# Attention value products by head: two 64-column products in place of one 128-column product, and one copy per result

## Chip, core and metric

The kernel runs on one core of a Trainium2 chip. The metric is the device time of one execution in microseconds (us); less is better. Engines: TensorE (PE in the profile, with its weight loads as PEld), VectorE (DVE), ScalarE (ACT), GpSimd (POOL) and SyncE (SP, which issues most loads).

## What is computed

The reference is a two-layer encoder over 512 positions and 1024 channels. Each layer adds three branches to the residual and then a squared-ReLU MLP. Branch C, which the change touches, is windowed grouped-query attention with 8 query heads of 64 columns and 2 key/value heads; a block of 128 queries sees its own block of 128 keys and the two beside it:

```
scores = jnp.einsum('bnqhgd,bnkhd->bnhgqk', qb, kb).astype(jnp.float32) * (C_HDIM ** -0.5)
...
p = p / (jnp.sum(p, axis=-1, keepdims=True) + jnp.exp(sink_l - m))
o = jnp.einsum('bnhgqk,bnkhd->bnqhgd', p.astype(v.dtype), vb)
```

The change concerns the last line, probabilities times values. All of it is in float32.

## The kernel before

A layer first projects its input (the matmuls of lines 201 to 203 and 407 to 409), then works out the branches. Branch A is a gated recurrence in four heads. Branch B is a gated product, whose columns `fill` merges one after another (`merge_b`, tiles gz and yB). Branch C is attention. After that come the branches' output projections (yC, yA), the output projection (wo) and the MLP (up and the d tiles). Large products are made from three matmuls of split operands, 128 weight columns by 512 moving columns each.

Branch C takes its 8 heads as four pairs, j = 0 to 3: head j of the first key/value head with head 4 + j, which belongs to the second. The pair's 2 × 64 channels stand on the 128 partitions of one tile: the first head ("lo64") on partitions 0 to 63, the second ("hi64") on 64 to 127. The values cv have keys on partitions and the two value heads side by side in 128 columns. For each pair and each block n of 128 queries, `c_scores` (line 903) makes the scores of both heads (lines 914 and 915), the softmax (917 to 925) and the scaled probabilities, head 0 on DVE (928) and then head 1 on ACT (930). `c_out` (line 933) turns them and multiplies them by the values:

- line 943: PE transposes each key block of head 0 into a PSUM tile, then those of head 1;
- line 944: ACT copies each head's turned blocks to the SBUF tile pT, which holds, per key block, head 0's 128 query columns and then head 1's;
- line 948: for each of the 2 or 3 key blocks b, one matmul with all 128 value columns as weights and both heads' 256 columns moving, summed over b in the PSUM tile po (128 partitions × 256 columns);
- line 950: two ACT copies, each of 64 partitions × 128 columns, take the two useful quarters of po to yc: head 0's value columns with head 0's probabilities, and the same of head 1. The other two quarters, each head's probabilities with the other's values, are not used.

There are 32 such results, 4 pairs × 4 query blocks × 2 layers. The end blocks see 2 key blocks and the inner ones 3, so 10 per pair and 80 in all. In float32 each non-transposing matmul of the program stands in the profile as two rows, so line 948 has 160.

Branch A's heads (`a_head`, line 528) run beside this. Their line 540 makes products with 64 weight columns and 64 moving columns, two for each of four position tiles, written to partitions 0 to 63 and 64 to 127 by turns, eight per call of `attn`; each head calls it eight times.

The order on each engine is not written by hand. The kernel is traced in program order with priorities (`later` puts a part behind others), and a scheduler at build time places instructions of the branches between one another on every engine. PSUM tiles come from four pools of two banks; the turned probabilities, po and some others share pool "s". The tile pT has one buffer, so the next result's copies of line 944 wait for the products that read it.

Of the kernel before, what the change touches and what calls it, by code (L numbers as in the profile page):

```python
# [12 lines left out]
P = 128  # L13
# [46 lines left out]
def trunk(tc, xT, xt, ws, vec, fnb, bsb, snk, wst, rope, cmask, amask, ident, out):  # L60
    nc = tc.nc
# [30 lines left out]
    def nm(s):  # L92
        ctr[0] += 1
        return f"{s}_{ctr[0]}"

    def T(tag, name, dt=F32):
        where = part[HOME[tag]] if tag in HOME else sb
        return where.tile([P, S], dt, tag=tag, bufs=SLOTS[tag], name=nm(name))
# [17 lines left out]
    def PT(tag, name):  # L116
        return ps.tile([P, S], F32, tag="p_" + tag, bufs=BANKS[tag], name=nm(name))
# [561 lines left out]
    for l in range(DEPTH):  # L679
# [194 lines left out]
        lo64, hi64 = slice(0, 64), slice(64, 128)  # L874
# [15 lines left out]
        cv = T("ch", "cvt")  # L890
# [10 lines left out]
        yc = []  # L901
# [31 lines left out]
        def c_out(j, n, lo_, nb, Ps):  # L933
            if n == 0:
                yc.append(T("l", "yc"))


            pT = part["br"].tile([P, 3, 2, P], F32, tag="pT", bufs=1, name=nm("pT"))
            for h in range(2):
                pt = PT("s", "pT")  # L940
                for b in range(nb):
                    c = slice(b * P, (b + 1) * P)
                    nc.tensor.transpose(pt[:, c], Ps[h][:, c], id_t)
                nc.scalar.copy(pT[:, :nb, h], pt[:, :nb * P].rearrange("p (a b) -> p a b", a=nb))
            po = PT("s", "po")
            for b in range(nb):
                kb = (lo_ + b) * P
                nc.tensor.matmul(po[:, 0:2 * P], cv[:, kb:kb + P], pT[:, b].rearrange("p a b -> p (a b)"), start=b == 0, stop=b == nb - 1)  # L948
            for h, r in enumerate((lo64, hi64)):
                nc.scalar.copy(yc[j][r, n * P:(n + 1) * P], po[r, h * P:(h + 1) * P])  # L950

        def gates(tag, i, fl):

# [12 lines left out]
        def c_run(j):  # L966
            nonlocal prev
            with later(15000):
                qs = c_q(j)
                for n in range(4):  # L970
                    cur = c_scores(j, n, qs)
                    if prev is not None:
                        c_out(*prev)
                    prev = cur
# [13 lines left out]
        with later(15000):  # L988
            c_out(*prev)
# [281 lines left out]
```

## Time and profile before

| What | Value |
|---|---|
| Three runs | 1712.42, 1714.54, 1716.99 us; median 1714.54 us |
| Profiled execution, its own time | 1714.73 us |
| Span of its instructions | 1712.9 us, 22985 instructions |
| Mean granted clock of TensorE | 0.994 |

In the profile, a row of a group of instructions gives line, engine, operation, output tile<-input tiles, shape and count, then the busy time in us and the mean of one in ns, and behind the second bar the idle time of the engine before them and what ended it. For PE "128\*64" means 128 rows and 64 weight columns in use. A row of the timeline gives start and duration in us, and "x4" where equal instructions were merged: the duration then runs from the first one's start to the last one's end. PE's matmuls overlap, so what one costs is the distance from its start to the start of the next. A row of the windows gives, for a stretch, each engine's busy time with the number of instructions, then the granted PE clock, the DMA share and the transfer rate.

Branch C's products run in two stretches, from about 250 to 440 us in the first layer and from about 1100 to 1284 us in the second.

### The profile page before, as it was taken

To read this page: it belongs to the slowest core of one execution; us is meant where nothing else is said; L and a number is where in the kernel's file an instruction comes from. 1 tells how busy PE (TensorE), PEld (TensorE's weight loads), DVE (VectorE), ACT (ScalarE), POOL (GpSimd) and SP (SyncE) were. 2 spreads that over 40 slices of the span, in tenths; PEclk is the share of its full clock that TensorE was granted. 3 is DMA by queue.
4 is the path that set the end of the run, shared out by engine and by line. 5 is a ranking of instruction groups with operands and counts; after the bars stand their busy time and mean duration, and the time that the engine had idled before them with its cause. 6 is when DMAs were issued, how large, how long until landed. Compare 5 with 4: busy or idle time off the path is not lost.

```text
span 1712.9 us, 22985 instructions
## 1 busy us (share of the span) xinstructions
PE 1675.5 (98%) x8536; PEld 1379.8 (81%) x8536; DVE 1285.7 (75%) x2049; ACT 1009.5 (59%) x1691; POOL 122.0 (7%) x198
## 2 busy tenths in 40 slices
PE   7999999999999999999999999999999999999997
PEld 5788887887778888888878888888877788888886
DVE  7896987678465758687889869876875567676877
ACT  6565578677325645455666666877882355545464
POOL 1021000000320000000010210000004100000001
PEclk9999999999999999999999999999999999999999
DMA  8243222231465233332333332322216453232311
GB/s 318 77 148 108 87 87 87 87 105 56 156 237 184 88 122 98 100 111 99 123 123 98 136 106 84 105 87 87 98 44 248 158 185 99 99 112 85 124 61 50
DMA packets 58144, 199.85 MB, mean 117 GB/s; under 512 B 7888, under 2 KB 8144, under 8 KB 58032
## 3 DMA queue, kind: packets, MB, share of 16 engines
q1 hardware_dynamic: 44496, 154.46, 27.0%
q0 software_dynamic: 13248, 43.40, 6.9%
q8 instruction: 67, 1.10, 0.3%
q10 hardware_dynamic: 288, 0.52, 0.1%
q14 instruction: 45, 0.37, 0.1%
HBM read 177.38 MB, written 20.97 MB: 116 GB/s over the span
## 4 chain that ended last, share of the span: by engine, by line
PE 86%; ACT 5%; DVE 4%; DMA 2%; issue 1%; POOL 1%; SPq 0%; POOLq 0%; ACTq 0%; DVEq 0%
PE up L202 7%; PE up L201 7%; PE up L203 7%; PE dA L408 3%; PE dA L407 3%; PE dA L409 3%; PE po L948 2%; PE gA L407 2%; PE wo L244 2%; PE at L540 2%; PE dC L408 2%; PE dC L407 2%; PE dC L409 2%; PE gA L409 2%; PE gA L408 2%; PE wo L243 2%
## 5 line engine op out<-in xcount | busy, mean ns | idle before, releaser
L196 ACT CAST wh<-wq 128x1024 fp32r<-128x1024 f32 x196 | 206.3, 1052 | 213.5 <-PE dA L408 49.2
L196 ACT CAST wh<-wr 128x1024 fp32r<-128x1024 f32 x171 | 179.6, 1050 | 247.5 <-PE up L202 88.7
L197 DVE TENSOR_TENSOR wl<-wr,wh 128x1024 fp32r<-128x1024 f32 x171 | 208.8, 1221 | 154.2 <-ACT wh L196 153.3
L197 DVE TENSOR_TENSOR wl<-wq,wh 128x1024 fp32r<-128x1024 f32 x196 | 239.0, 1221 | 89.0 <-ACT wh L196 87.8
L202 PE MATMUL up<-xl,wh 128*128 128x512 f32 x512 | 199.1, 389 | 0.0
L203 PE MATMUL up<-xh,wl 128*128 128x512 f32 x512 | 199.0, 389 | 0.0
L201 PE MATMUL up<-xh,wh 128*128 128x512 f32 x512 | 198.6, 389 | 0.0
L201 PEld LDWEIGHTS up<-xh,wh 128*128 128x128 f32 x512 | 96.1, 188 | 20.1
L203 PEld LDWEIGHTS up<-xh,wl 128*128 128x128 f32 x512 | 96.1, 188 | 20.0
L202 PEld LDWEIGHTS up<-xl,wh 128*128 128x128 f32 x512 | 96.1, 188 | 19.7
L407 PE MATMUL dA<-wh,sh 128*128 128x512 f32 x256 | 99.7, 390 | 0.0
L408 PE MATMUL dA<-wh,sh 128*128 128x512 f32 x256 | 99.6, 389 | 0.0
L409 PE MATMUL dA<-wl,sh 128*128 128x512 f32 x256 | 92.6, 389 | 0.0
L580 DVE TENSOR_TENSOR ex<-ex 128x512 f32<-128x512 f32 x112 | 74.8, 685 | 4.7 <-ACT kt L556 4.2
L407 PEld LDWEIGHTS dA<-wh,sh 128*128 128x128 f32 x256 | 48.0, 188 | 10.0
L409 PEld LDWEIGHTS dA<-wl,sh 128*128 128x128 f32 x256 | 48.1, 188 | 10.0
L408 PEld LDWEIGHTS dA<-wh,sh 128*128 128x128 f32 x256 | 48.1, 188 | 9.9
L263 POOL TENSOR_TENSOR rs<-ms,mhalf_t 128x4 f32<-128x4 f32 (+2 forms) x15 | 18.5, 1233 | 493.6 <-DVE ms L261 484.3
L554 DVE TENSOR_TENSOR qt<-qt,q 128x512 f32<-128x512 f32 x56 | 38.4, 686 | 18.9 <-ACT qt L553 18.5
L553 ACT ACTIVATE qt<-ex 128x512 f32<-128x512 f32 x56 | 37.7, 674 | 24.5 <-DVE ex L580 19.4
L251 ACT CAST sh<-sf 128x512 fp32r<-128x512 f32 x64 | 39.6, 619 | 19.4 <-DVE sf L372 17.5
L201 PE MATMUL gz<-xh,wh 128*128 128x512 f32 x128 | 50.7, 396 | 0.0
(405 smaller groups left out, 4343.1 us busy)
## 6 DMA issues: line engine op xcount, KB each, us to landing
wr<-in_ws_dram SPq DMA_DIRECT2D x171, 512.0 KB, 3.4
wq<-in_ws_dram SPq DMA_DIRECT2D x112, 512.0 KB, 4.3
thd<-zt POOLq DMA_DIRECT2D x32, 256.0 KB, 2.5
th<-thd POOLq DMA_DIRECT2D x32, 256.0 KB, 3.4
mgd<-mg POOLq DMA_DIRECT2D x16, 256.0 KB, 2.6
mcd<-th POOLq DMA_DIRECT2D x16, 256.0 KB, 3.1
mC<-mcd POOLq DMA_DIRECT2D x16, 256.0 KB, 7.2
mB<-mgd POOLq DMA_DIRECT2D x16, 256.0 KB, 6.6
```

The source lines that it names most:

```text
L196: nc.scalar.copy(hi, raw)
L197: nc.vector.tensor_tensor(lo, raw, hi.bitcast(F32), ALU.subtract)
L201: nc.tensor.matmul(pt, whi, xhi, start=first, stop=False)
L202: nc.tensor.matmul(pt, whi, xlo, start=False, stop=False)
L203: nc.tensor.matmul(pt, wlo, xhi, start=False, stop=last)
L251: nc.scalar.copy(hi, src)
L407: nc.tensor.matmul(pt, xh[:, t], hi[:, c], start=start and k == 0, stop=False, skip_group_check=True)
L408: nc.tensor.matmul(pt, xl[:, t], hi[:, c], start=False, stop=False, skip_group_check=True)
L409: nc.tensor.matmul(pt, xh[:, t], lo[:, c], start=False, stop=k == 3, skip_group_check=True)
L553: nc.scalar.activation(qt.rearrange(shp, b=nb, h=2), e_q, AF.Exp)
L554: nc.vector.tensor_tensor(qt, qt, q, ALU.mult)
L580: nc.vector.tensor_tensor(o_ap, o_ap, ap_of(ex, i_, [[istep, 2]] + z), ALU.add)
```

## The change

For each key block, two products take the place of one. Each has its own head's 64 value columns as weights and its own 128 probability columns moving, and writes its own 64 partitions of po, columns 0 to 127: head 1 to partitions 64 to 127, head 0 to 0 to 63. Head 1, whose probabilities are scaled, turned and copied after head 0's, comes first. The unused quarters of po are no longer made. One copy of 128 partitions × 128 columns takes the result to yc.

```diff
             for b in range(nb):
                 kb = (lo_ + b) * P
-                nc.tensor.matmul(po[:, 0:2 * P], cv[:, kb:kb + P], pT[:, b].rearrange("p a b -> p (a b)"), start=b == 0, stop=b == nb - 1)
-            for h, r in enumerate((lo64, hi64)):
-                nc.scalar.copy(yc[j][r, n * P:(n + 1) * P], po[r, h * P:(h + 1) * P])
+                for h, r in ((1, hi64), (0, lo64)):
+                    nc.tensor.matmul(po[r, 0:P], cv[:, kb + h * 64:kb + h * 64 + 64], pT[:, b, h], start=b == 0, stop=b == nb - 1, skip_group_check=True)
+            nc.scalar.copy(yc[j][:, n * P:(n + 1) * P], po[:, 0:P])
```

The products are now of line 949 and the copy stays on line 950. The scheduler places them anew, and other instructions with them.

First place, PE in the first layer, the second result of branch C (po: the products; at: branch A's 64-column products; pT: turned probabilities; sc: scores; gz: a column of branch B's gate). Before:

```order
L201 MATMUL gz_3028<-xh_164,wh_3024 128x512
L540 MATMUL at_2229<-qt_2224,kt_2227 64x64 x8
L540 MATMUL at_2242<-q_2220,key_2239 64x64 x8
L948 MATMUL po_2070<-pT_2059,cvt_1965 128x256 x3
L943 MATMUL pT_2099<-id_t,sc_2043 128x128 x3
L914 MATMUL sc_2449<-k_398_1949,q_511_2436 128x256
```

The same place now:

```order
L201 MATMUL gz_3051<-xh_172,wh_3047 128x512
L949 MATMUL po_2071<-pT_2060,cvt_1965 64x128 x2
L540 MATMUL at_2234<-qt_2229,kt_2232 64x64 x8
L540 MATMUL at_2247<-q_2225,key_2244 64x64 x8
L949 MATMUL po_2071<-pT_2060,cvt_1965 64x128 x4
L943 MATMUL pT_2102<-id_t,sc_2044 128x128 x3
```

The three wide products became six narrow ones, and the scheduler put them around two groups of branch A's narrow products.

Second place, PE at the end of branch C in the first layer (kT and stp: the last steps of branch A's fourth head; yC: branch C's output projection). Before:

```order
L948 MATMUL po_2871<-pT_2860,cvt_1965 128x256 x3
L943 MATMUL pT_2900<-id_t,sc_2844 128x128 x3
L540 MATMUL at_3742<-qt_3737,kt_3740 64x64 x8
L595 MATMUL kT_3762<-id_t,kd_3760 128x128 x3
L943 MATMUL pT_2905<-id_t,sc_2849 128x128 x3
L600 MATMUL stp_3768<-vt_464,kT_3766 128x128
L600 MATMUL stp_3768<-vt_466,kT_3766 128x128
L600 MATMUL stp_3768<-vt_540,kT_3766 128x128
L595 MATMUL kT_3781<-id_t,kd_3779 128x128 x3
L948 MATMUL po_2910<-pT_2899,cvt_1965 128x256 x3
L943 MATMUL pT_3079<-id_t,sc_2883 128x128 x2
```

The same place now:

```order
L540 MATMUL at_3732<-qt_3727,kt_3730 64x64 x8
L949 MATMUL po_2890<-pT_2879,cvt_1965 64x128 x6
L943 MATMUL pT_2921<-id_t,sc_2863 128x128 x3
L540 MATMUL at_3749<-qt_3744,kt_3747 64x64 x8
L943 MATMUL pT_2926<-id_t,sc_2868 128x128 x3
L949 MATMUL po_2931<-pT_2920,cvt_1965 64x128 x6
L943 MATMUL pT_3102<-id_t,sc_2904 128x128 x2
L540 MATMUL at_3766<-qt_3761,kt_3764 64x64 x8
L943 MATMUL pT_3106<-id_t,sc_2909 128x128 x2
L595 MATMUL kT_3786<-id_t,kd_3784 128x128 x3
L949 MATMUL po_3110<-pT_3101,cvt_1965 64x128 x4
```

Before, a group of branch A's narrow products, two groups of its kT and one of its stp stood between the last two three-block products of branch C; now only one narrow group and transposes stand between them, and kT comes ahead of the last two-block product alone.

Third place, ACT at the end of branch C in the second layer (yc: the copy of a result; kd, ms, qd, kT: branch A's fourth head; yh: the rounded yc, which yC needs). Before:

```order
L572 COPY at_11079<-own_11080 64x4x64 x2
L586 ACTIVATE ms_11216<-ex_11030 128x2
L592 ACTIVATE kd_11219<-ex_11030 128x384
L571 COPY at_11079<-at_11201 64x4x64 x2
L609 ACTIVATE qd_11235<-ex_11030 128x384
L587 ACTIVATE ms_11216<-ex_11030 128x2
L592 ACTIVATE kd_11238<-ex_11030 128x384
L950 COPY yc_10268<-po_10355 64x128 x2
L944 COPY pT_10523<-pT_10524 128x2x128
L597 COPY kT_11225<-kT_11221 128x384
```

The same place now:

```order
L950 COPY yc_10310<-po_10400 128x128
L944 COPY pT_10570<-pT_10571 128x2x128
L944 COPY pT_10570<-pT_10575 128x2x128
L553 ACTIVATE qt_11244<-ex_11078 128x512
L556 ACTIVATE kt_11247<-ex_11078 128x512
L572 COPY at_11127<-own_11128 64x4x64 x2
L950 COPY yc_10310<-po_10579 128x128
L251 CAST yh_11647<-yc_10310 128x512
L586 ACTIVATE ms_11264<-ex_11078 128x2
L592 ACTIVATE kd_11267<-ex_11078 128x384
```

The last two results of branch C are copied once each, and now ahead of branch A's kd instead of behind it.

Over the whole program, the 64-column matmuls of PE (lines 540 and 949) stand in 80 unbroken stretches where there were 58: 45 of line 540 alone, 21 of line 949 alone, 14 of both. Behind 45 of the 80 stretches comes a group of 128×128 transposes (lines 943, 595, 889), which was so behind 17 of the 58.

## The prediction

> **What bounds the kernel now.** I read the page first: the span, the busy shares and the chain that ended last.
>
> ```profile
> span 1712.9 us, 22985 instructions
> PE 1675.5 (98%) x8536; PEld 1379.8 (81%) x8536; DVE 1285.7 (75%) x2049; ACT 1009.5 (59%) x1691; POOL 122.0 (7%) x198
> ...
> PE 86%; ACT 5%; DVE 4%; DMA 2%; issue 1%; POOL 1%; SPq 0%; POOLq 0%; ACTq 0%; DVEq 0%
> ```
>
> PE is busy 98% of the span and holds 86% of the chain. A mean hides stages, so next the windows over the two stretches that hold branch C (time, then PE, PEld, DVE, ACT and POOL busy with their counts, PE clock, DMA share, GB/s):
>
> ```profile
> 180.00:420.00 240.00, 239.37 (x1557) 197.52 (x1556) 189.93 (x414) 167.98 (x347) 11.92 (x19) 1.00 0.27 88
> 420.00:440.00 20.00, 14.98 (x96) 12.20 (x96) 10.52 (x27) 13.72 (x37) 0.00 (x0) 0.83 0.09 27
> 1030.00:1260.00 230.00, 229.53 (x1469) 188.96 (x1469) 186.49 (x381) 172.33 (x338) 11.36 (x18) 1.00 0.27 89
> 1260.00:1285.00 25.00, 21.14 (x172) 15.97 (x172) 19.45 (x50) 22.81 (x63) 0.59 (x1) 1.00 0.11 32
> ```
>
> These are two regimes. In the long windows PE idles 0.6 of 240 us and 0.5 of 230 us, while DVE and ACT are at 70 to 81%: PE time is the time there, and a PE microsecond removed is one off the end. In the two ends of branch C, the second and fourth rows, PE idles 5.0 and 3.9 us, and the granted clock is 0.83 in the first of them. There the chain of softmax, transposes, copies and branch A's last head sets the time, and ACT is busy 22.81 of 25 us in the fourth. The groups by line tell what the changed lines hold:
>
> ```profile
> L948 PE MATMUL po<-pT,cvt 128*128 128x256 f32 x160 | 43.1, 398 | 0.5 <-ACT pT L944 0.5
> ...
> L950 ACT COPY yc<-po 64x128 f32<-64x128 f32 x64 | 16.5, 257 | 7.7 <-PE po L948 7.0
> ```
>
> **The products.** The 398 ns are a latency. The cost is the distance between starts, from the timeline of PE:
>
> ```profile
> 249.40 0.61 PE L623 MATMUL av<-st,qd 128*128 128x128 f32 x4
> 249.85 0.39 PE L623 MATMUL av<-vt,at 128*128 128x128 f32 x2
> ...
> 250.29 1.03 PE L948 MATMUL po<-pT,cvt 128*128 128x256 f32 x4
> 251.16 0.49 PE L943 MATMUL pT<-id_t,sc 128*128 128x128 f32 x3
> 251.41 0.36 PE L914 MATMUL sc<-k,q 128*128 128x256 f32 x1
> ```
>
> Four rows of line 948 take 251.16 − 250.29 = 0.87 us, 0.2175 each; a key block has two rows, so 0.435. A row with 128 moving columns takes (249.85 − 249.40) / 4 = 0.1125. The new block has four rows of that length, two per head. Laid end to end they cost 0.45, slightly more than now. They save only if the two heads run at the same time, each in its half of the weight columns. No row here has 64 weight columns and 128 moving ones; the nearest is branch A's line 540, whose products go to the two halves by turns:
>
> ```profile
> 261.59 0.64 PE L540 MATMUL at<-q,key 128*64 128x64 f32 x16
> ...
> L540 PE MATMUL at<-qt,kt x896: 222/222/271, 185.2 to 1276.7; 128*64 128x64 f32 x180
> ```
>
> Sixteen rows run 0.64 us, the last of them 0.222, so the last starts 0.42 after the first. A row of 64 moving columns should take half of 0.1125, 0.056, and fifteen in sequence 0.84. They take half of that, so two run at once. The last pair starts seven pairs behind the first and its second row half a step later at most, so a pair costs between 0.42 / 7.5 and 0.42 / 7, say 0.058: about the price of one row. At 128 columns a pair costs between 0.1125 (full overlap) and 0.225 (none). I take 0.1125, since the form differs from line 540's in length alone. A block is then 0.225 and saves 0.21, and 80 blocks save **16.8 us**.
>
> **The switch.** Line 540's rows also show a price. One group among wide matmuls, and one followed by transposes:
>
> ```profile
> 277.74 0.39 PE L202 MATMUL f<-xl,wh 128*128 128x512 f32 x1
> 277.97 0.39 PE L203 MATMUL f<-xh,wl 128*128 128x512 f32 x1
> ...
> 278.42 0.39 PE L202 MATMUL f<-xl,wh 128*128 128x512 f32 x1
> 278.74 0.69 PE L540 MATMUL at<-qt,kt 128*64 128x64 f32 x16
> 279.35 0.50 PE L203 MATMUL f<-xh,wl 128*128 128x512 f32 x1
> 279.69 0.39 PE L201 MATMUL f<-xh,wh 128*128 128x512 f32 x1
> ...
> 348.02 0.39 PE L203 MATMUL yB<-yh,wl 128*128 128x512 f32 x1
> 348.34 0.69 PE L540 MATMUL at<-qt,kt 128*64 128x64 f32 x16
> 348.95 0.55 PE L943 MATMUL pT<-id_t,sc 128*128 128x128 f32 x3
> 349.26 0.42 PE L914 MATMUL sc<-k,q 128*128 128x384 f32 x1
> ```
>
> Wide rows follow each other at 0.23 (277.97 − 277.74). From 278.42 to 279.69 are 1.27 us; the work in it is two wide rows, 0.455, and eight pairs, 0.464, so 0.35 are left over. From 348.02 to 349.26 are 1.24; the work is one wide row, 0.23, eight pairs, 0.464, and the three transposes, 0.25 as at 251.16, so 0.30 are left over. Each way in and out of 64-column work leaves PE empty, for 0.30 with transposes behind it and 0.35 otherwise. The new order has 80 such stretches for 58, and 45 of them end in transposes for 17. That is 45 × 0.30 + 35 × 0.35 = 25.8 us against 17 × 0.30 + 41 × 0.35 = 19.5, so **6.3 us** more. The fourteen stretches that hold products of both kinds pay once for both; were every result of branch C a stretch of its own, 32 × 0.30 = 9.6 would go.
>
> The Trainium skill, TensorEngine Tiling (Array Packing), section Tiling Modes, speaks against the change here: it says that changing the tiling mode drains TensorE. It gives no price. An estimate from the ~128 cycles of drain that TensorE: Matmul & The Clock Gate states (Step-by-step: what each phase is for) is 53 ns at 2.4 GHz, 0.11 us per stretch for two drains; 22 more stretches would cost 2.3 us. By that the sum below would end at 1698.2 us. The rows show about three times as much per stretch, and the measurement decides.
>
> **The copy.** The nearest row to one copy of 128 partitions × 128 columns out of PSUM is branch A's square; two copies as they are now stand beside it:
>
> ```profile
> L628 ACT ACTIVATE asq<-av x32: 257/278/288, 250.6 to 1290.2; 128x128 f32<-128x128 f32 x32
> ...
> 259.07 0.52 ACT L950 COPY yc<-po 64x128 f32<-64x128 f32 x2
> ...
> 428.61 0.51 ACT L950 COPY yc<-po 64x128 f32<-64x128 f32 x2
> ...
> 440.32 0.53 ACT L950 COPY yc<-po 64x128 f32<-64x128 f32 x2 [1.22 <-PE po L948]
> ...
> 1260.69 0.52 ACT L950 COPY yc<-po 64x128 f32<-64x128 f32 x2
> ...
> 1283.14 0.53 ACT L950 COPY yc<-po 64x128 f32<-64x128 f32 x2 [0.33 <-PE po L948]
> ...
> 1280.20 0.44 PE L943 MATMUL pT<-id_t,sc 128*128 128x128 f32 x2 [1.22 <-ACT yc L950]
> ```
>
> 0.52 becomes about 0.27, so each result saves 0.25 us of ACT, 8 us in 32. In the long windows this is worth nothing, for ACT is idle a quarter of them and PE is what ends last. In the two ends it is on the chain: at 1280.20 PE waited 1.22 us for that very copy, since its PSUM bank is wanted by the next transposes. Three results are copied in the first end (the first and the last of them at 428.61 and 440.32) and five in the second (1260.69 to 1283.14); 8 × 0.25 = **2.0 us**. It is between 0, if another wait is late instead, and 2.0.
>
> **Head 1 first.** The wide product already waits for both heads' copies, head 1's being the later. The first narrow product waits for the same one, and the second finds its data there. No engine gets a new wait, nothing queues behind it, and no DMA hangs on it: priced at nothing. Were head 0 first, PE could stop in the middle of a stretch; that is the cover this order gives. What the scheduler moved besides is priced at nothing as well: the loads on SP stand as before, and POOL, on which a few stores, loads and powers change places, is busy 11.9 of 240 us in the first long window.
>
> **The sum.** It is made against the profiled execution, 1714.73 us (span 1712.9 and 1.8 around it), 0.2 above the median of the runs. 1714.7 − 16.8 + 6.3 − 2.0 = **1702.2 us**.
>
> **Rivals.**
>
> 1. *No overlap at 128 columns* (slower). If the halves cannot both stream 128 columns, a block costs 0.45, the products rise by 80 × 0.015 = 1.2 us, and the switches stay: 1714.7 + 1.2 + 6.3 − 2.0 = 1720.2 us. It decides above 0.38 us per block, where the saving no longer pays the switches (4.3 / 80 = 0.054 below 0.435). Against it stand line 540's pairs; for it, that those have only 64 columns. Chance 0.04.
> 2. *Half overlap.* A block lies midway between 0.225 and 0.45, at 0.3375, and 80 save 7.8: 1714.7 − 7.8 + 6.3 − 2.0 = 1711.2 us. Line 540 shows no such loss. Chance 0.06. The Trainium skill's Measured speedup vs the span model (TensorE: Matmul & The Clock Gate) has 2.38 for three column tiles, an estimate of 1.59 for two; a block would be 0.28, and the sum about 1707. Line 540's 0.058 for a pair does not bear that out.
> 3. *The ends grow.* The new order packs the last results of branch C in the first layer close together, and each needs ACT between transposes and products. The ends hold 8.9 us of PE idle time and 20 × (1 − 0.83) = 3.4 us of lost clock, 12.3 together. Half as much again, without the ACT gain: 1714.7 − 10.5 + 6.2 = 1710.4 us, within 0.3%. The rows for it:
>
> ```profile
> 428.76 0.55 PE L595 MATMUL kT<-id_t,kd 128*128 128x128 f32 x3 [1.52 <-ACT kd L592]
> ...
> 432.40 1.65 PE L600 MATMUL stp<-vt,kT 128*128 128x128 f32 x6 [2.67 <-ACT kT L597]
> ```
>
>    The first end idles behind ACT, long enough that the clock falls. Chance 0.08.
> 4. *The ends shrink.* The same rows say what could go: branch A's kT and stp stood between branch C's last products, which waited behind stp's 2.67 us. In the new order the products come ahead of stp, and in the second layer ahead of kd, with yC work behind. Half of the 12.3 gone: 1714.7 − 10.5 − 6.2 = 1698.0 us. Chance 0.20.
>
> **How the numbers follow.** The forecast keeps 0.62. A measurement of this kernel can tell about 0.3%, 5.1 us, from no change. Forecast and rival 4 are faster: 0.82; rivals 2 and 3 lie within 5.1 us: 0.14; rival 1 is slower: 0.04. The range goes from 1697.0, a little beyond rival 4, to 1710.5, which takes in rival 3, switches at 9.6 and a copy that saves nothing; it leaves out rivals 1 and 2, 0.10, and the outer part of rival 4.
>
> **What would show it.** In the new profile: 320 rows of line 949 with 64 weight columns; in a lone stretch of 12 the last start about 0.62 us after the first, against 1.24 for rival 1; 0.30 left over around it; line 950 with 32 copies near 0.27; PE still idle for less than 1 us in the long windows, which end about 5 us earlier in each layer; no clock below 1 at the end of the first layer for rival 4. The prediction is wrong if the pairs do not overlap, if the long windows show PE idle, or if the ends change by more than 6 us.

## The result, and the profile after

| | before | changed |
|---|---|---|
| Median | 1714.62 us (6 runs) | 1700.32 us (6 runs, 1698.89 to 1703.90) |
| Ratio | 1 | 0.9921, 95% interval 0.9909 to 0.9934 |
| Profiled execution, its span | 1714.73, 1712.9 us | 1699.31, 1697.5 us |

The change makes the kernel faster by 14.3 us of the medians; the forecast was 12.5. The interval of the ratio is a gain of 11.3 to 15.6 us, so the forecast lies within what was measured. Of the six runs of the changed kernel, the two with a mean granted clock of 0.992 took 1702.55 and 1703.90 us, the four with 0.994 or 0.995 took 1698.89 to 1700.37.

The page of the changed kernel begins so:

```profile
span 1697.5 us, 23267 instructions
PE 1662.9 (98%) x8696; PEld 1366.7 (81%) x8696; DVE 1284.7 (76%) x2049; ACT 996.7 (59%) x1659; POOL 122.9 (7%) x198
...
PE 81%; issue 7%; ACT 5%; DVE 4%; POOL 1%; DMA 1%; SPq 0%; POOLq 0%; ACTq 0%; DVEq 0%
```

PE is still the bound. It has 160 instructions more and is busy 12.6 us less, of the 15.4 us by which the span is shorter. The share of "issue" in the chain differs between runs of this case (4% in e2, 8% in e8) and is not read here. The view of the tile po shows the new products and the copy (shortest, median and longest in ns, then first and last start):

```profile
L949 PE MATMUL po<-pT,cvt x320: 272/273/325, 249.2 to 1262.7; 128*64 128x128 f32 x160
L950 ACT COPY yc<-po x32: 239/256/281, 259.5 to 1264.1; 128x128 f32<-128x128 f32 x32
```

320 rows of 64 weight columns and 32 copies of 0.26 us stand there, as the prediction named them. The timeline of PE at a stretch of 12 product rows that stands alone:

```profile
273.56 0.39 PE L203 MATMUL f<-xh,wl 128*128 128x512 f32 x1
273.88 0.88 PE L949 MATMUL po<-pT,cvt 128*64 128x128 f32 x12
274.69 0.44 PE L943 MATMUL pT<-id_t,sc 128*128 128x128 f32 x2
274.88 0.42 PE L915 MATMUL sc<-kl,q 128*128 128x384 f32 x1
```

The twelve rows run 0.88 us and one lasts 0.272, so the last starts 0.61 after the first. The prediction wanted 0.62 for pairs that run at once and 1.24 for pairs that do not. From 273.56 to 274.88 are 1.32; one wide row at 0.23, six pairs at 0.1125 and two transposes from 274.69 to 274.88 make 1.095, so 0.22 is left for this stretch, less than the 0.30 that the prediction named.

The windows, as they were read of before, show the two long stretches and the two ends of branch C:

```profile
180.00:420.00 240.00, 239.20 (x1648) 194.73 (x1646) 192.63 (x424) 167.27 (x347) 11.93 (x19) 1.00 0.27 89
420.00:440.00 20.00, 16.83 (x126) 13.95 (x127) 12.29 (x23) 10.39 (x32) 2.71 (x5) 0.91 0.31 108
1030.00:1260.00 230.00, 228.31 (x1577) 185.74 (x1577) 188.74 (x403) 174.22 (x355) 11.94 (x19) 1.00 0.27 88
1260.00:1285.00 25.00, 22.70 (x157) 18.39 (x152) 15.22 (x29) 11.93 (x32) 4.21 (x8) 1.00 0.37 137
```

The long windows are as full as before: PE idles 0.8 us in one, and 1.7 in the other, where the prediction named less than 1. The second of them now holds work of the end as well, for branch C's last copy is at 1264.1 instead of 1283.14; from 1030 to 1250 PE idles 0.2. The first end idles 3.2 us for 5.0 and has a clock of 0.91 for 0.83; but the ends come earlier now, so the same clock times hold other work. The first end in the timeline of PE:

```profile
420.09 0.69 PE L540 MATMUL at<-qt,kt 128*64 128x64 f32 x16 [0.60 <-ACT kt L556]
...
421.82 0.88 PE L949 MATMUL po<-pT,cvt 128*64 128x128 f32 x12 [0.57 <-ACT pT L944]
...
423.84 0.69 PE L540 MATMUL at<-qt,kt 128*64 128x64 f32 x16 [0.77 <-DVE qt L554]
...
427.02 0.66 PE L949 MATMUL po<-pT,cvt 128*64 128x128 f32 x8 [1.03 <-ACT pT L944]
427.90 1.65 PE L600 MATMUL stp<-vt,kT 128*128 128x128 f32 x6 [0.23 <-ACT kT L597]
```

The waits of 1.52 and 2.67 us that the prediction quoted for kd and kT have become several short ones; the last products wait 1.03 for their copy and stp 0.23.

Behind the second end, where PE was busy without a break before (from 1285 to 1295 us), something new stands in the changed kernel:

```profile
1287.89 1.08 PE L635 MATMUL oT<-id_t,ao 128*128 128x128 f32 x4 [2.14 <-DVE ao L631]
...
1290.34 0.63 PE L244 MATMUL yA<-wh,yl 128*128 128x512 f32 x1
1290.77 0.63 PE L245 MATMUL yA<-wl,yh 128*128 128x512 f32 x1
```

PE waits 2.14 us for an output of branch A (ao), and the wide rows behind it start 0.43 apart instead of 0.23. The clock records of the trace, from which the profile takes the granted clock, show half clock from 1288.0 to 1291.4. In the first end half clock lasts from 427.8 to 431.2 now, where it lasted from 430.5 to 437.3 before. So PE has 6.8 us at half clock around branch C in both kernels, before all of it in the first layer.

### The profile page after: what moved, and what is told of

Same layout as the page of the kernel before. It is cut to its first block, busy times and chain, and to the rows that moved or that the text cites. A ratio compares the mean times of both kernels' runs of the same rounds, so it can differ in the third digit from the quotient of the medians.

```text
span 1697.5 us, 23267 instructions
## 1 busy us (share of the span) xinstructions
PE 1662.9 (98%) x8696; PEld 1366.7 (81%) x8696; DVE 1284.7 (76%) x2049; ACT 996.7 (59%) x1659; POOL 122.9 (7%) x198
## 4 chain that ended last, share of the span: by engine, by line
PE 81%; issue 7%; ACT 5%; DVE 4%; POOL 1%; DMA 1%; SPq 0%; POOLq 0%; ACTq 0%; DVEq 0%
PE up L201 7%; PE up L202 7%; PE up L203 7%; PE dA L408 3%; PE dA L407 3%; PE dA L409 3%; PE wo L244 2%; PE dC L407 2%; PE dC L408 2%; PE dC L409 2%; PE wo L245 2%; PE wo L243 2%; PE at L540 1%; PE gz L201 1%; PE gz L203 1%
## 5 line engine op out<-in xcount | busy, mean ns | idle before, releaser
L263 POOL TENSOR_TENSOR rs<-ms,mhalf_t 128x4 f32<-128x4 f32 (+2 forms) x15 | 19.4, 1295 | 480.1 <-DVE ms L261 477.1
L201 PE MATMUL f<-xh,wh 128*128 128x512 f32 x128 | 50.6, 396 | 0.2 <-DVE z L693 0.2
```

What stands on the lines that cost most here:

```text
L201: nc.tensor.matmul(pt, whi, xhi, start=first, stop=False)
```

## The experiments

A ratio is to the kernel before on the same chip; the changed kernel's is 0.9921. "Us above the changed kernel" is the difference of the two ratios times 1714.6. Each ratio is known to about 0.0013, so such a difference is known to about 3 us; where less is claimed, it is read from the traces row by row.

Four questions: do the products overlap (e1, e2), what does a switch cost (e9, e10), what is a copy worth (e3, e5, e11), and what do the head and the order on PE do (e4, e6, e7, e8, e12).

### The products: e2 and e1

e2 splits the product by head but not by columns: both heads keep all 128 weight columns, and there are two copies as before.

```
+ for h in (1, 0):
+     nc.tensor.matmul(po[:, h*P:(h+1)*P], cv[:, kb:kb+P], pT[:, b, h], start=b == 0 and h == 1, stop=b == nb-1, ...)
+ for h, r in enumerate((lo64, hi64)):
+     nc.scalar.copy(yc[j][r, n*P:(n+1)*P], po[r, h*P:(h+1)*P])
```

> One product per head, but with all 128 value columns as weights and 128 moving columns, and the two copies as before: the split into two products without the halves. Theory: 320 rows at 0.1125 are 36.0 us against 34.8 before, no more stretches of 64-column work than before (58), so 1.2 us slower, ratio 0.998 to 1.003. Rival (the gain lies in splitting the product by head, so that the first part can start sooner, or in the scheduler's new order): faster than before by several us, ratio 0.993 to 0.997.

Measured: 1712.44 us, ratio 0.9992 (0.9983 to 1.0001). Two instructions for one gain nothing without the halves.

e1 keeps the changed products and copy, and swaps the two loops:

```
- for b in range(nb):
-     for h, r in ((1, hi64), (0, lo64)):
+ for h, r in ((1, hi64), (0, lo64)):
+     for b in range(nb):
```

> The same narrow products, but all key blocks of head 1 first and then all of head 0, so that neighbours in PE's order write the same half of the partitions; only at the seam do the two halves meet. Theory (two heads run at once, one in each half of the weight columns): 320 rows of 0.1125 us in sequence less one row at each of 32 seams, 32.4 us against 17.9 with alternating heads, so about 14.5 us more than the changed kernel: ratio to before 0.999 to 1.002. Rival A (what runs at once are the two rows of one and the same product): nothing changes, ratio about 0.992. Rival B (the gain came from the single copy or from the new order at the ends of branch C): nothing changes either, ratio about 0.992.

Measured: 1706.54 us, ratio 0.9957 (0.9942 to 0.9971), 6.2 us above the changed kernel: neither the theory's number nor the rivals' came. The timeline of PE in e1, for a result of two key blocks and one of three (the same result as the 0.88 above):

```profile
249.67 0.66 PE L949 MATMUL po<-pT,cvt 128*64 128x128 f32 x8
...
274.83 1.14 PE L949 MATMUL po<-pT,cvt 128*64 128x128 f32 x12
```

The changed kernel's first result, of two blocks, in the same view:

```profile
249.17 0.66 PE L949 MATMUL po<-pT,cvt 128*64 128x128 f32 x8
```

With two blocks, four rows of head 1 stand ahead of four of head 0, and the eight still take 0.66, as when they stand by turns. With three blocks six stand ahead of six, and the twelve take 1.14, 0.26 more; 16 inner results make 4.2 of the 6.2 us; the rest stays open, as e1 has an order of its own from the scheduler (81 stretches of 64-column work for 80). The starts of the rows in e1's trace, in us, show how far it reaches:

```
two blocks:    249.667 249.680   249.828 249.840   249.937 249.949   250.046 250.058
three blocks:  274.832 274.992 275.101 275.107 275.210 275.267 275.319 275.376 275.428 275.485 275.594 275.703
```

With two blocks all are pairs, the fifth row of the list beside the first. With three, two rows start alone, 0.11 to 0.16 apart, then the other half comes in beside the third, and two rows are alone at the end. So rival A is out, for the first two rows, which belong to one product, start 0.16 apart. The halves do run at once, but the theory was wrong that only the rows at the seam meet: the rows need not stand by turns. The second half comes in four rows ahead, and what stands further back waits.

### The switch: e9 and e10

From here on some kernels have the order on the engines held fixed. The list of the order that the scheduler gave is written into the kernel, and each instruction of an engine is put behind the one before it in the list:

```
for a, b in zip(order[:-1], order[1:]):
    tc.add_manual_dep(own[b], own[a].name, why, reason="order")
```

Such an edge sets the place and adds no instruction: e6, held so, has 23267 as the changed kernel has. e6 and e10, held so, also take the changed kernel's time; the changed kernel with its own order held and nothing else changed was not run. As the same row then stands at the same place in two traces, the difference of its starts shows where two kernels part. For all pairs of this kind, the start in one less the start in the other, in us, at the row that begins at the time named in the second kernel of the pair:

```
start in the second kernel:  185   250   300   400   440   520  1030  1100  1250  1290  1360
e9 against the changed       0.5   2.3   4.4   6.8   7.9   7.9   8.4   9.5  14.0  13.6  14.0
e10 against the changed     -0.1  -0.1  -0.4  -0.9  -0.6  -0.6  -0.2  -0.2  -1.4  -0.7  -0.4
e5 against the changed       0.4   0.6   2.2   2.2   3.9   3.9   3.7   3.6   3.8   5.1   6.5
e11 against the changed      0.1   0.1   0.6   0.6   1.1   1.1   1.0   1.0   1.2   2.2   3.3
e6 against the changed       1.8   2.0   2.0   1.9   0.5   0.6   0.4   0.2   0.2   0.4   1.6
e8 against the changed       1.0   1.5   7.2   9.4  10.3  10.3  10.1  10.0  14.3  16.0  17.3
e7 against before           -0.8  -0.8  -1.0  -4.0  -5.9  -6.4  -6.4  -6.1  -9.9 -12.2 -12.5
e12 against before           0.1   0.5  -0.3  -3.3  -4.9  -5.0  -5.1  -5.1  -8.9  -9.5  -6.7
```

Each line of this table is one execution set against one, and part of a difference is the granted clock. From 185 to 1600 us the clock records of the traced executions show these stretches at half clock, in us and in order of time:

```
before   6.8              e4   3.4              e9    6.8  3.4
changed  3.4  3.4         e5   6.9  6.8         e10   6.8  3.4
e1       3.4  3.4  6.8    e6   6.8              e11   3.5  6.8
e2       3.4              e7   6.9              e12   6.8  3.4  3.4
e3       3.4  3.4  10.2   e8   3.4  6.8
```

A PE that is busy throughout loses half of such a stretch. So in the table up to 3.4 us of what e5 and e12 lose, and up to 1.7 of what e8, e9, e10 and e11 lose, can be the clock's.

e9 moves one wide row into each of 43 stretches and changes nothing else. On PE, for the first such stretch:

```
- L203  L540 x8            L201
+       L540 x4  L203  L540 x4  L201
```

> The changed kernel with every engine held in its own order, and on PE one thing moved: at 43 of the 80 stretches of 64-column work the wide row that stood just ahead of the stretch now stands in its middle. Nothing is added; the stretches become 123. Theory, 0.35 us per stretch with wide rows behind: 43 x 0.35 = 15.0 us, so 1715.4 us, ratio 0.999 to 1.002. Rival, 0.11 us per stretch (the estimate that the prediction worked out from TensorE: Matmul & The Clock Gate in the Trainium skill): 4.7 us, 1705 us, ratio 0.994 to 0.9955.

Measured: 1716.07 us, ratio 1.0009 (1.0000 to 1.0018), 15.1 us above the changed kernel for 15.0 expected. The timeline of PE at that stretch in e9:

```profile
203.53 0.39 PE L202 MATMUL cq<-xl,wh 128*128 128x512 f32 x1
203.85 0.45 PE L540 MATMUL at<-qt,kt 128*64 128x64 f32 x8
204.23 0.50 PE L203 MATMUL cq<-xh,wl 128*128 128x512 f32 x1
204.66 0.45 PE L540 MATMUL at<-qt,kt 128*64 128x64 f32 x8
205.04 0.50 PE L201 MATMUL cq<-xh,wh 128*128 128x512 f32 x1
```

From 203.53 to 205.04 are 1.51 us; two wide rows are 0.455 and eight pairs 0.464, so 0.59 are left over for two stretches. In the table the 43 further stretches cost 14.0 us, 0.33 each; the 40 of them that lie in the two long stretches of branch C, away from half clock, cost 0.31 to 0.32 each. The estimate of 0.11 that the prediction worked out from the Trainium skill is refuted. What the Trainium skill says, that a change of the tiling mode drains TensorE (TensorEngine Tiling (Array Packing), Tiling Modes), agrees in so far as each way in and out costs time, 0.31 to 0.35 us here; whether a drain is where that time goes, no run shows.

e10 goes the other way: 12 pairs of neighbouring stretches are made one. One of them:

```
- L540 x8  L203 L201 L202 L203  L949 x6
+ L203 L201 L202 L203  L540 x8  L949 x6
```

> The changed kernel with every engine held in its own order, and on PE 12 pairs of neighbouring stretches of 64-column work made one, by moving the 1 to 4 rows between them ahead of both or behind both: 68 stretches for 80. Theory, 0.30 to 0.35 us per stretch: 12 x 0.32 = 3.8 us less, 1696.5 us, ratio 0.989 to 0.991. Rival, that the rows moved wait for their data instead: 0.992 to 0.994.

Measured: 1701.31 us, ratio 0.9923 (0.9911 to 0.9936): nothing gained. The table says why. Nine of the twelve merges lie in the two long stretches and work there: three give 0.8 us by 400, six give 1.2 between 1030 and 1250, which is 0.2 to 0.3 each where 0.32 was expected. At the two ends it is taken back, by waits, and in the first end by half clock too (6.8 us for 3.4). Between 1250 and 1254, PE's timeline in e10:

```profile
1249.15 0.55 PE L943 MATMUL pT<-id_t,sc 128*128 128x128 f32 x3
1250.28 0.50 PE L243 MATMUL yC<-wh,yh 128*128 128x512 f32 x1 [0.59 <-DVE mx L917]
```

In the changed kernel a group of line 540 stood behind those transposes and filled the time in which PE now waits 0.59. Here a switch removed was worth its price only where the row that was moved had not covered a wait.

### The copy: e3, e5 and e11

All three have the changed products and two copies of 64 partitions:

```
- nc.scalar.copy(yc[j][:, n*P:(n+1)*P], po[:, 0:P])
+ for r in (lo64, hi64):
+     nc.scalar.copy(yc[j][r, n*P:(n+1)*P], po[r, 0:P])
```

e3 leaves the order to the scheduler.

> The changed products with two copies of 64 partitions each, as before, in place of the one: the copy alone is undone. Theory: 0 to 2.0 us slower than the changed kernel, since ACT is off the path but for the two ends of branch C: ratio to before 0.992 to 0.9935. Rival (the copy carries the gain, because it frees the PSUM bank earlier for the next transposes everywhere): half of the gain or more is lost, ratio 0.996 or above.

Measured: 1708.80 us, ratio 0.9971 (0.9960 to 0.9983), 8.6 us above: the rival's number. But the scheduler had given PE another order as well (82 stretches of 64-column work for 80), and its trace has 17.0 us at half clock for 6.8, up to 5.1 us of lost time. So e5 holds PE's order.

> The changed kernel with two copies of 64 partitions per result, as in e3, but with every instruction of PE held in exactly the changed kernel's order (the order is given to the scheduler as a list). Theory, that the second copy is worth what the prediction gave it, up to 2 us in the two ends of branch C, and that the rest of e3's 8 us came from the scheduler's other order: ratio 0.992 to 0.994. Rival, that the second copy itself costs e3's 8 us: 0.996 to 0.998.

Measured: 1705.36 us, ratio 0.9946 (0.9934 to 0.9959), 4.3 us above, between the two. Of the 6.5 in the table 1.6 come between 250 and 300, at one place. The timeline of ACT and PE there in e5:

```profile
266.80 1.28 ACT L492 ACT_TABLE_LOAD   x1
...
268.09 0.21 ACT L492 ACTIVATE lb<-lb 128x8 f32<-128x8 f32 x1
268.21 0.52 ACT L951 COPY yc<-po 64x128 f32<-64x128 f32 x2
...
268.78 0.55 PE L943 MATMUL pT<-id_t,sc 128*128 128x128 f32 x3 [1.16 <-ACT yc L951]
```

The copies stand behind a table load of 1.28 us in ACT's queue, and PE waits 1.16 for them. The rows in the changed kernel's timeline:

```profile
264.45 0.25 ACT L950 COPY yc<-po 128x128 f32<-128x128 f32 x1
...
266.92 0.55 PE L943 MATMUL pT<-id_t,sc 128*128 128x128 f32 x3
```

There the copy is made 2.2 us ahead. At this place the loss is ACT's order, not the copy's length. So e11 holds all five engines.

> As e5, the changed kernel with two copies of 64 partitions per result, but with all five engines held in the changed kernel's order, the second copy directly behind the first. Theory of the prediction, 8 results in the two ends at 0.25 us: 2.0 us, 1702.3 us, ratio 0.9925 to 0.9938. Rival 1, that e5's 5 us are the second copy's own: ratio 0.9942 to 0.9955. Rival 2, that a second copy costs nothing: 0.9915 to 0.9925.

Measured: 1702.59 us, ratio 0.9934 (0.9920 to 0.9947), 2.2 us above for 2.0 expected. The interval alone does not refute rival 2; the table speaks against it: 1.1 us by the end of branch C in the first layer, and from 1.0 to 2.2 in the second by 1290. The 1.1 after that stands in e6 as well, which has one copy: both have 6.8 us at half clock near 1290 where the changed kernel has 3.4. It is not counted. As e6 differs from the changed kernel by up to 2.0 us on the way, the 2.2 is less exact than it looks.

### The head and the order: e4, e6, e7, e8 and e12

e4 puts head 0's product first.

```
- for h, r in ((1, hi64), (0, lo64)):
+ for h, r in ((0, lo64), (1, hi64)):
```

> The changed kernel with head 0's product ahead of head 1's in each key block: the order of the heads alone is undone. Theory: the overlap is the same; PE may stop after the first product to wait for head 1's copy, 0.4 to 0.5 us at worst in each of 32 results where the copy is not done by then, so between nothing and a few us: ratio 0.992 to 0.995. Rival (head 1 first carries much of the gain): ratio 0.996 or above, with PE waiting for line 944 inside the stretches.

Measured: 1709.99 us, ratio 0.9978 (0.9968 to 0.9987), 9.8 us above: the rival's number. PE's timeline in e4:

```profile
267.49 0.55 PE L943 MATMUL pT<-id_t,sc 128*128 128x128 f32 x3
267.97 0.43 PE L949 MATMUL po<-pT,cvt 128*64 128x128 f32 x2
268.33 0.50 PE L201 MATMUL f<-xh,wh 128*128 128x512 f32 x1
...
274.83 0.87 PE L949 MATMUL po<-pT,cvt 128*64 128x128 f32 x10
```

Head 0's first product depends on head 0's copy alone, so the scheduler places it 6.9 us ahead of the ten other rows of its result, as a stretch of its own. There are 97 stretches for 80, which at 0.33 to 0.35 is 5.6 to 6.0 us, and the rows torn off run without a partner. e6 has e4's edit with PE held in the changed kernel's order.

> The changed kernel with head 0's product ahead of head 1's in each key block, as in e4, but with PE held in the changed kernel's order otherwise: head 0's product stands exactly where head 1's stood and the reverse, so there are 80 stretches of 64-column work and not e4's 97. Theory, that e4 lost by the 17 more stretches that the scheduler made of it, and that the head that comes first is worth nothing by itself: ratio 0.991 to 0.9935. Rival, that PE loses time by stopping in the middle of a stretch for the later copy: 0.995 to 0.998.

Measured: 1701.00 us, ratio 0.9920 (0.9907 to 0.9934): as the changed kernel. On the chip it is the same which head comes first; the order decides through what the scheduler makes of it.

e7 is the changed kernel with PE held in the order of the kernel before, each pair standing where the wide product stood; e8 is the kernel before with PE in the changed kernel's order.

> The changed kernel (two products per key block, one copy), with PE held in the order of the kernel before: each pair of products stands where the wide product stood. 78 stretches of 64-column work. Theory, that products and switches make the gain wherever they stand: 1714.6 - 16.8 + 5.7 - up to 2 = 1701.5 to 1703.5, ratio 0.992 to 0.994. Rival, that a third or more of the gain is the scheduler's new order: ratio 0.995 to 0.998.

> The kernel before (one wide product per key block, two copies), with PE held in the order of the changed kernel: the wide product stands where the first of the pair stands now. Theory, that the new order by itself is worth nothing: ratio 0.999 to 1.002. Rival, that a third or more of the gain is the order: 0.994 to 0.998.

Measured: e7 1706.89 us (1702.19 to 1709.13), ratio 0.9962 (0.9949 to 0.9976), 7.0 us above the changed kernel; e8 1716.44 us, ratio 1.0013 (1.0004 to 1.0022). For e7 the rival's number came; for e8 the theory's. The new order by itself is no gain, yet the new products without it gain half. As PE's order alone lets the others move (e8 loses 5.7 of its 17.3 us between 250 and 300, where e5 had its stall), e12 is e7 with all five engines in the order of before.

> As e7, the changed kernel in the order of the kernel before, but with all five engines held in that order: the pair of products stands where the wide product stood, the one copy where the first of the two stood. 78 stretches of 64-column work for 58. Theory, the prediction's sum with no rearrangement at all: 1714.3 - 16.8 + 5.7 - 2.0 = 1701.2 us, ratio 0.991 to 0.994. Rival, that the order of PE is what the products lack here, as in e7: 0.995 to 0.998.

Measured: 1707.08 us, ratio 0.9959 (0.9947 to 0.9972): the rival's number again. The table shows where the sum holds. At 1290 e12 is 9.5 us ahead of before. Then 2.8 are given back by 1360. The timeline there in e12, and the same rows in before:

```profile
1314.67 0.66 PE L1023 MATMUL mT<-id_t,mC 128*128 128x128 f32 x4 [0.67 <-DVE mB L1028]
...
1315.55 1.04 ACT L196 CAST wh<-wr 128x1024 fp32r<-128x1024 f32 x1 [7.00 <-DMA wr<-in_ws_dram]
1316.50 0.61 ACT L251 CAST mgh<-mB 128x512 fp32r<-128x512 f32 x1
...
1317.17 0.73 PE L243 MATMUL wo<-wh,mgh 128*128 128x512 f32 x2 [1.84 <-ACT mgh L251]
```

```profile
1323.29 1.04 ACT L196 CAST wh<-wr 128x1024 fp32r<-128x1024 f32 x1 [4.82 <-PE mT L1023]
...
1324.52 0.62 ACT L251 CAST mgh<-mB 128x512 fp32r<-128x512 f32 x1 [0.18 <-DMA mB<-mgd]
1324.54 0.65 PE L1023 MATMUL mT<-id_t,mC 128*128 128x128 f32 x4 [1.09 <-DVE mB L1028]
1325.19 0.73 PE L243 MATMUL wo<-wh,mgh 128*128 128x512 f32 x2
```

Before, the weights landed at 1323.19 by the trace, the row of PE that ACT's cast also waits for ended at 1323.23, and PE found its operand there. In e12 PE comes 9.9 us earlier (1314.67), but the weights land at 1315.45, only 7.7 us earlier: ACT idles 7.00 us until then, its next cast follows, and PE waits 1.84 for that. Behind this wait the clock is at one half from 1318.0 to 1321.4, as the distance of the wide rows shows, 0.43 for 0.23:

```profile
1319.85 0.63 PE L245 MATMUL wo<-wl,mgh 128*128 128x512 f32 x1
1320.28 0.63 PE L244 MATMUL wo<-wh,mgl 128*128 128x512 f32 x1
```

About 1.5 of the 2.8 us go at the wait, and the rest behind it, most of it at half clock. The gain meets a transfer that does not come earlier by as much. e7's profiled execution has no such loss (12.2 us ahead at 1290 and 12.5 at 1360) and is the fastest of its five runs, with a mean clock of 0.995. The other four have 0.991 to 0.993, which over 1700 us is 3.4 to 6.8 us of full clock, and they are 3.5 to 6.9 us longer. So lost clock could explain the spread; whether they stalled at this place no trace shows.

## Why the prediction was nearly right

**The products: right.** 16.8 us forecast. A pair costs 0.11 as taken from line 540, rival 1 (1.24 in the lone stretch) and rival 2 are out, and e2 shows that it is the halves that save. By the median distance of starts in the traces, a row of before takes 0.216 and a pair now 0.109: 160 × 0.216 − 160 × 0.109 = 17.1 us.

**The switch: right.** 0.30 and 0.35 were read from two stretches; 43 more cost 0.31 to 0.35 each (e9), and those removed gave 0.2 to 0.3 (e10). Those of e9 have wide rows behind them. Over the changed kernel's own stretches the medians are 0.29 with transposes behind and 0.35 with wide rows, so the 6.3 stands.

**The copy: right in fixed order.** 2.0 forecast, 2.2 measured (e11), known to about 3 us from the times and from one pair of executions row by row. Its two places were the two ends, as said, apart from 0.5 between 250 and 300.

**Head 1 first: right on the chip, wrong as a cover.** It was priced at nothing, and e6 shows nothing. But "PE could stop in the middle of a stretch" is not what head 0 first costs. The scheduler tears the products apart, and that is 9.8 us (e4).

**The order: the step that failed.** "What the scheduler moved besides is priced at nothing as well" does not hold. In the order of before the terms of the sum come out by the end of branch C: e12 is 9.5 us ahead at 1290, where 17.1 less 20 more stretches at 0.33 leave 10.5. But the whole run gains 7 us there and 14.3 with the new order. Set between the first row of line 540 and the first row of the up matmuls, the first layer takes 346.3 us before, 341.2 in e12 and 337.5 changed; the second 337.4, 335.8 and 331.9.

In these two layers together PE idles 14.8 us before, 15.9 in e12 and 12.1 in the changed kernel, and it is at half clock for 6.8, 13.6 and 6.8 us. So of the 7.6 us that e12 is longer than the changed kernel there, 3.8 are waits of PE and up to 3.4 are lost clock: the order decides how long PE waits at the ends of branch C and behind them. It need not cost both layers alike, for e7's traced execution, in the old order on PE alone, takes 340.7 and 331.1, in the second layer no more than the changed kernel.

In the changed kernel's own order the sum holds. Of the 14.4 us that the two layers gain, 11.7 are PE's busy time, for 16.8 − 6.3 = 10.5 forecast, and 2.7 are its idle time, where the copy's 2.0 was priced. But in the order of before the same products, switches and copy gain about 6.5 us less over the whole run, the difference of e12 and the changed kernel. That the scheduler would make an order in which the sum holds was not argued in the prediction; in this the forecast was lucky. Another 1.2 us of the profiled gain lie ahead of the first row of line 540, where nothing was changed; e6, in the changed kernel's order, gets there 1.8 us later than the changed kernel.

**Rival 4, that the ends shrink, came in part:** from the first row of line 540 to the first row of the up matmuls PE idles 5.5 us for 7.9 in the first layer, but 6.6 for 6.8 in the second, and 3.4 of the 6.8 us at half clock went from the first end to behind the second. It had 0.20 beside 0.62. **Rival 3 did not come.**

**What stays open:** how much of the 6.5 us belongs to the order, and how much to the clock that the traced executions happened to get, for the clock differs between executions of one kernel and one of each was traced; and why the weights' load holds PE up in e12 and not in e7's trace.

## What to carry to other kernels

Two products that use half of the weight columns each ran at once here and cost as one (0.109 us a pair), but every stretch of such work paid about a third of a microsecond for the way in and out: count the stretches before the rows. In a kernel whose order a scheduler sets, compare one edit only with the order held on every engine; left free, the second copy seemed to cost 8.6 us where it costs 2.2, and the head that comes first 9.8 where it costs nothing. A gain in a full stretch is kept only if what comes behind it, here a weight load, can come earlier too. Before a difference of a few us between two traces is put down to an edit, compare their stretches at half clock.

## What was not expected of the hardware

The two halves of the weight columns do not keep step. In e1, PE's list at 261.61 has six rows of head 1's products, then groups of line 540, then six rows of head 0's. The timeline shows rows of lines 949 and 540 starting by turns:

```profile
261.61 0.54 PE L949 MATMUL po<-pT,cvt 128*64 128x128 f32 x3
261.88 0.27 PE L540 MATMUL at<-qt,kt 128*64 128x64 f32 x1
261.99 0.27 PE L949 MATMUL po<-pT,cvt 128*64 128x128 f32 x1
261.99 0.22 PE L540 MATMUL at<-qt,kt 128*64 128x64 f32 x1
262.10 0.27 PE L949 MATMUL po<-pT,cvt 128*64 128x128 f32 x1
```

Rows of line 540 start while product rows ahead of them in the list have yet to start: read so, a half that has nothing to do takes its next row ahead of the other's, four rows ahead in the stretches of e1 above. Rows of one half follow each other at 0.11 (261.99 to 262.10). The Trainium skill (TensorE: Matmul & The Clock Gate, Step-by-step: what each phase is for) says that matmuls stay in program order; within a half the records agree, between the halves they do not.
